# FFN products by one level of Strassen's scheme, and score products pinned in pairs, in a four-block fp32 trunk

## Chip, cores and metric

The kernel runs on one core of one Trainium2 chip, in one launch. The metric is the device time in microseconds of that core; 1996.79 us is the median of three runs (1996.62 to 1997.18).

## What is computed

The input x is 512 tokens of 1024 features in fp32. There are two layers; each adds an FFN, a mixer and a second FFN to x. The mixer of layer 0 is a causal differential attention with 8 heads, that of layer 1 a gated MLP over chunks of 128 tokens (gMLP). Cut to what matters here:

```
def _swiglu_ffn(x, w_gate_up, w_down):          # 1024 x 5632 and 2816 x 1024
    g, u = jnp.split(x @ w_gate_up, 2, axis=-1)
    return (jax.nn.silu(g) * u) @ w_down

for i in range(2):
    x = x + 0.5 * _swiglu_ffn(_rmsnorm(x, ffn1_norm[i]), ffn1_w_gate_up[i], ffn1_w_down[i])
    x = x + mixer(_rmsnorm(x, mix_norm[i]))     # attention in layer 0, gMLP in layer 1
    x = x + 0.5 * _swiglu_ffn(_rmsnorm(x, ffn2_norm[i]), ffn2_w_gate_up[i], ffn2_w_down[i])
```

In the attention, the scores of a head are computed for two components (cc) of 64 features and for blocks of 128 queries, against the keys up to the block's end.

## The kernel before

x lies in SBUF as eight tiles `x[k]` of 128 features by 512 tokens. Products run on TensorE in fp32r form, and each fp32 operand is split into a high part (a copy by ScalarE) and a low part (a subtraction by VectorE), so that `mm3` (L126) issues three matmuls for one product. Names: PE is TensorE, DVE VectorE, ACT ScalarE, POOL GpSimd, SP the engine that issues every load; an f tile is 128 of the 2816 hidden features, a k tile 128 of the 1024 features of x.

The stages follow one another: f0, attention, f1 (layer 0), f2, gMLP, f3 (layer 1). An FFN (`ffn`) goes through two halves of 11 f tiles. For each tile j it loads 1 MB of gate and up weights (`load`, L113), splits them in two pieces of 1024 columns (`split`, L118, with L122 on ACT and L123 on DVE), and multiplies them by the halves `xh`, `xl` of the 8 k tiles, for gate and up: 48 matmuls of 512 columns (L127 to L129). `gated` (L232) scales by the norm's row factor `rb`, takes silu and splits the result h. After a half, 8 down blocks of 704 KB (33 matmuls each) are added to `x[m]` (L285), and in the second half the next norm's `add` makes the new halves and squares (L158, L159, L166, L167).

The norm's factor comes late: `rstd` issues four products with a vector of ones (L173) behind the fourth k tile of the first f tile (the second in f0), and `rows` (L195, L199) turns the factor into a 128x512 tile `rb` on all partitions. Nothing before `gated` needs it.

The framework's scheduler sets the order in each engine's queue by readiness. In the attention and the gMLP, `interleave` (L311) picks the order of tasks by a table of estimated times. `scores` (L481) writes, for one head and one block, three products (L495) per component, alternating between the components, and a mask product (L499); the scheduler is free to move them.

Of the kernel before, what the change touches and what calls it, by code (L numbers as in the profile page):

```python
# [17 lines left out]
P = 128  # L18
# [35 lines left out]
def kernel(  # L54
# [28 lines left out]
    wraw = ctx.enter_context(tc.tile_pool(name="wraw", bufs=2))  # L83
    wsplit = ctx.enter_context(tc.tile_pool(name="wsplit", bufs=5))
# [7 lines left out]
    xh = [acts.tile([P, S], F32R, name=f"xh{k}") for k in range(KT)]  # L92
    xl = [acts.tile([P, S], F32R, name=f"xl{k}") for k in range(KT)]
# [49 lines left out]

    class Norm:


        def __init__(self, layer, kind, name):
            self.g0 = C_GAIN + (layer * 3 + kind) * KT
            self.name = name
            self.acc = stat.tile([P, S], F32, tag="sqacc", name=name + "acc", bufs=1)  # L150

# [28 lines left out]
        def rows(self, r):  # L180
# [6 lines left out]
            for part, half in ((f32(rh), "h"), (rl, "l")):  # L187
# [671 lines left out]
```

## Time and profile before

| | us | 
|---|---|
| median of three runs | 1996.79 |
| the profiled execution, device time | 1996.96 |
| its span, first to last instruction | 1995.2 |
| PE busy | 1984.2 |
| DVE busy | 1032.3 |
| ACT busy | 670.0 |

The span is what the instructions cover; the device time is a little longer. An engine's busy time is the union of its instructions' spans. A busy PE means only that some matmul was under way, since matmuls are pipelined: the starts of two in a row tell the price of one better than a duration does. TensorE's granted clock was 1.0 in every slice, its upper level. A time of landing is that from a DMA's issue to its end.

### The profile page before, as it was taken

What the parts mean: (1) busy time and instruction counts of PE and PEld (TensorE: products, weight loads), DVE (VectorE), ACT (ScalarE), POOL (GpSimd) and SP (SyncE); (2) the same over time, 40 slices, a digit from 0 to 9 for tenths busy, and PEclk for the clock granted to TensorE, in tenths of its full rate; (3) what the DMA queues carried; (4) which work ended last, traced back from release to release, by engine and by line L of the source; (5) the groups of instructions that cost most, each with busy time, mean ns of one, the idle gap of its engine ahead of it and who ended that gap; (6) DMA issues with size and microseconds to landing.
All of it is one profiled execution on the core that took longest, in us unless ns stands there. A gap on an engine that the chain in (4) does not pass through costs nothing.

```text
span 1995.2 us, 22193 instructions
## 1 busy us (share of the span) xinstructions
PE 1984.2 (99%) x9034; PEld 1629.9 (82%) x9034; DVE 1032.3 (52%) x1663; ACT 670.0 (34%) x960; POOL 2.6 (0%) x11
## 2 busy tenths in 40 slices
PE   8999999999999999999999999999999999999999
PEld 7888888877778888888888888888888888888887
DVE  7433444567778443444544334445586564434442
ACT  5222323355554322222423223233333242222321
POOL 0000000000000000000000000000000000000000
PEclk9999999999999999999999999999999999999999
DMA  5223222211112222322322232234332222223222
GB/s 193 99 73 120 100 86 94 105 64 64 55 52 85 89 81 95 126 84 74 127 87 90 88 127 85 79 103 146 115 116 85 89 102 88 83 94 127 85 78 81
DMA packets 32934, 190.34 MB, mean 95 GB/s; under 512 B 3776, under 2 KB 4160, under 8 KB 16576
## 3 DMA queue, kind: packets, MB, share of 16 engines
q1 hardware_dynamic: 32832, 188.93, 27.0%
q8 instruction: 71, 1.16, 0.2%
q14 instruction: 31, 0.25, 0.0%
HBM read 186.82 MB, written 2.10 MB: 95 GB/s over the span
## 4 chain that ended last, share of the span: by engine, by line
PE 98%; DVE 1%; ACT 1%; DMA 0%; SPq 0%; issue 0%; ACTq 0%
PE f2p L127 4%; PE f3p L127 4%; PE f3p L128 4%; PE f2p L129 4%; PE f3p L129 4%; PE f2p L128 4%; PE f1p L127 4%; PE f1p L128 4%; PE f1p L129 4%; PE f0p L127 4%; PE f0p L129 4%; PE f0p L128 4%; PE f3dp L127 2%; PE f2dp L129 2%; PE f1dp L127 2%; PE f0dp L129 2%
## 5 line engine op out<-in xcount | busy, mean ns | idle before, releaser
L235 DVE TENSOR_TENSOR f3g<-f3p,n5rbs 128x512 f32<-128x512 f32 x22 | 15.2, 691 | 58.7 <-PE f3p L129 58.7
L235 DVE TENSOR_TENSOR f1g<-f1p,n2rbs 128x512 f32<-128x512 f32 x22 | 15.2, 692 | 58.7 <-PE f1p L129 57.3
L235 DVE TENSOR_TENSOR f2g<-f2p,n3rbs 128x512 f32<-128x512 f32 x22 | 15.2, 691 | 58.7 <-PE f2p L129 58.7
L235 DVE TENSOR_TENSOR f0g<-f0p,n0rbs 128x512 f32<-128x512 f32 x22 | 15.2, 691 | 55.5 <-PE f0p L129 55.5
L158 ACT ACTIVATE xh<-x,sm 128x512 fp32r<-128x512 f32 x48 | 34.3, 718 | 17.8 <-DVE x L750 9.7
L159 DVE SCALAR_TENSOR_TENSOR xl<-x,sm,xh 128x512 fp32r<-128x512 f32 x48 | 35.6, 746 | 8.5 <-ACT xh L158 8.4
L285 DVE SCALAR_TENSOR_TENSOR x<-f3dp,x 128x512 f32<-128x512 f32 x16 | 11.1, 692 | 40.3 <-PE f3dp L129 40.3
L285 DVE SCALAR_TENSOR_TENSOR x<-f2dp,x 128x512 f32<-128x512 f32 x16 | 11.1, 692 | 29.3 <-PE f2dp L129 29.3
L285 DVE SCALAR_TENSOR_TENSOR x<-f1dp,x 128x512 f32<-128x512 f32 x16 | 11.1, 692 | 29.3 <-PE f1dp L129 29.3
L285 DVE SCALAR_TENSOR_TENSOR x<-f0dp,x 128x512 f32<-128x512 f32 x16 | 11.1, 692 | 29.3 <-PE f0dp L129 29.3
L750 DVE TENSOR_TENSOR x<-gop,x 128x512 f32<-128x512 f32 x24 | 16.5, 689 | 18.4 <-PE gop L129 18.4
L242 ACT ACTIVATE f3hh<-f3u 128x512 fp32r<-128x512 f32 x22 | 13.9, 633 | 28.1 <-DVE f3u L239 28.1
L242 ACT ACTIVATE f2hh<-f2u 128x512 fp32r<-128x512 f32 x22 | 13.9, 632 | 28.0 <-DVE f2u L239 28.0
L243 DVE TENSOR_TENSOR f3hl<-f3u,f3hh 128x512 fp32r<-128x512 f32 x22 | 15.2, 692 | 15.4 <-ACT f3hh L242 15.4
L243 DVE TENSOR_TENSOR f2hl<-f2u,f2hh 128x512 fp32r<-128x512 f32 x22 | 15.2, 692 | 15.4 <-ACT f2hh L242 15.4
L242 ACT ACTIVATE f1hh<-f1u 128x512 fp32r<-128x512 f32 x22 | 13.9, 632 | 27.3 <-DVE f1u L239 27.3
L243 DVE TENSOR_TENSOR f1hl<-f1u,f1hh 128x512 fp32r<-128x512 f32 x22 | 15.2, 692 | 14.7 <-ACT f1hh L242 14.7
L242 ACT ACTIVATE f0hh<-f0u 128x512 fp32r<-128x512 f32 x22 | 13.9, 632 | 26.5 <-DVE f0u L239 26.5
L593 DVE TENSOR_TENSOR x<-aop,x 128x512 f32<-128x512 f32 x32 | 21.5, 684 | 2.4 <-PE aop L129 2.3
L243 DVE TENSOR_TENSOR f0hl<-f0u,f0hh 128x512 fp32r<-128x512 f32 x22 | 15.2, 692 | 14.1 <-ACT f0hh L242 14.0
L730 ACT ACTIVATE gh<-gut 128x512 fp32r<-128x512 f32 x16 | 10.1, 631 | 33.7 <-DVE gut L729 33.7
L689 DVE TENSOR_TENSOR gut<-gup,n4rbs 128x512 f32<-128x512 f32 x16 | 11.0, 685 | 13.4 <-PE gup L129 13.4
(3643 smaller groups left out, 6456.7 us busy)
## 6 DMA issues: line engine op xcount, KB each, us to landing
f1gu<-in_gate_up_dram SPq DMA_DIRECT2D x22, 1024.0 KB, 4.8
f2gu<-in_gate_up_dram SPq DMA_DIRECT2D x22, 1024.0 KB, 4.8
f3gu<-in_gate_up_dram SPq DMA_DIRECT2D x22, 1024.0 KB, 4.8
f0gu<-in_gate_up_dram SPq DMA_DIRECT2D x21, 1024.0 KB, 4.8
f0d<-in_down_dram SPq DMA_DIRECT2D x16, 704.0 KB, 4.0
f1d<-in_down_dram SPq DMA_DIRECT2D x16, 704.0 KB, 4.0
f2d<-in_down_dram SPq DMA_DIRECT2D x16, 704.0 KB, 4.1
f3d<-in_down_dram SPq DMA_DIRECT2D x16, 704.0 KB, 4.1
```

Source lines behind the costliest of these rows:

```text
L127: nc.tensor.matmul(ps, sh, mh, start=start, stop=False)
L128: nc.tensor.matmul(ps, sh, ml, start=False, stop=False)
L129: nc.tensor.matmul(ps, sl, mh, start=False, stop=stop)
L158: nc.scalar.activation(xh[k], x[k], AF.Copy, scale=g)
L159: nc.vector.scalar_tensor_tensor(xl[k], x[k], g, f32(xh[k]), op0=ALU.mult, op1=ALU.subtract)
L235: nc.vector.tensor_tensor(gt, ps[0], rb, op=ALU.mult)
L242: nc.scalar.activation(a, ut, AF.Copy)
L243: nc.vector.tensor_tensor(b, ut, f32(a), op=ALU.subtract)
L285: nc.vector.scalar_tensor_tensor(x[m], pt, 0.5, x[m], op0=ALU.mult, op1=ALU.add)
L593: nc.vector.tensor_tensor(x[m], pt, x[m], op=ALU.add)
L689: nc.vector.tensor_tensor(ut, ps, rr["rb"], op=ALU.mult)
L750: nc.vector.tensor_tensor(x[m], pt, x[m], op=ALU.add)
```

## The change

*FFNs.* An FFN's first two f tiles of each half (`PLAIN` = 2: j = 0, 11, 1, 12) are still computed as before. For the others, tile i of the first half and tile i+11 of the second form a pair, k tiles k and k+4 another, and the two halves of 256 tokens a third. Such a 2×2×2 product is done with seven products in place of eight (Strassen's scheme in its form with shared sums): P1, P2, P6, P7, Q3, Q4 and Q5, on 256 columns. `Weigh` loads the four quarters of the weights a, b, c and d (512 KB each in a pair) and builds the sums: t = a + b on DVE (Q5); then, by DMAs issued from POOL that add to what lies in SBUF, t += c (P6), b += c (P7) and t += d (Q4). Each of the seven is split on ACT and DVE. `multiply` goes through 14 turns (7 products, gate and up) and accumulates them in three banks for each of gate and up: X takes P1, P6, P7 and Q4, Y takes Q5 and Q3, Z takes P2. Partial values are kept (`keep`) and the outputs formed from differences (L448 to L463).

The moving operand needs seven forms of 256 columns: `scaled` makes them for x (scaled by gain and `rb`, which is no longer applied afterwards for these pairs), `sums_of` and `halves_of` (one row of 1792 columns on ACT and one on DVE) make them for x and for h. The down products use the same scheme over pairs of f tiles, of output tiles and token halves, in chunks of 3, 3, 3 and 2 pairs with two parts each; chunks run between the gate and up pairs as soon as their h are there, the last two at the end. All FFN matmuls, with the norm's, are pinned in program order.

*Memory.* Loads are 512 KB in place of 1 MB and four buffers of them; `xh` and `xl` move to a shared pool of three homes; four split buffers instead of five; `QK_BUFS` 5 to 4 and `U_BUFS` 4 to 3.

*Scores.* All products of a group but the first, and the mask products, are pinned in program order.

Matmuls of an FFN go from 1584 of 512 columns to 192 of 512 and 2436 of 256. The last norm's `add`s of a part stand behind that part in program order.

```diff
 O_BUFS = 4
-U_BUFS = 4
-QK_BUFS = 5
+U_BUFS = 3
+QK_BUFS = 4
 BANKS = {"pp": 4, "ps": 3, "po": 1}
+HT = S // 2
+PLAIN = 2
+CHUNKS = ((0, 1, 2), (3, 4, 5), (6, 7, 8), (9, 10))
...
+    fixed = []
+    def matmul(ps, stationary, moving, start, stop, more=False):
+        mm = nc.tensor.matmul(ps, stationary, moving, start=start, stop=stop, skip_group_check=more)
+        if fixed:
+            tc.keep_in_program_order(mm)
...
+    class Weigh:
+        def __init__(self, pool, srcs, n, name):
+            self.n, self.name, self.done = n, name, {}
+            self.raw = {}
+            for q in "abcd":
+                self.raw[q] = t = wraw.tile([P, 1024], F32, tag="raw", name=f"{name}{q}")
+                for dst, src in srcs[q]:
+                    nc.sync.dma_start(t[:, dst], src)
+            t = self.raw["t"] = pool.tile([P, 1024], F32, tag="t", name=f"{name}t")
+            nc.vector.tensor_tensor(t[:, :n], self.raw["a"][:, :n], self.raw["b"][:, :n], op=ALU.add)
+        def more(self, to, by):
+            n = self.n
+            nc.gpsimd.dma_start(self.raw[to][:, :n], self.raw[by][:, :n], accum_op=ALU.add)
+        def take(self, prod):
+            if prod in self.done:
+                return self.done[prod]
+            if prod == "Q5":
+                src = "t"
+            elif prod == "P1":
+                src = "a"
+            elif prod == "P6":
+                self.more("t", "c")
+                self.done["P2"] = split(self.raw["d"], self.n, f"{self.name}P2")
+                src = "t"
+            elif prod == "P7":
+                self.more("b", "c")
+                src = "b"
+            elif prod == "Q4":
+                self.more("t", "d")
+                src = "t"
+            elif prod == "Q3":
+                src = "c"
+            self.done[prod] = split(self.raw[src], self.n, self.name + prod)
+            return self.done[prod]
     def ffn(layer, which, norm, nxt):
...
+        first = which == 0 and layer == 0
+        slot = {"P1": 0, "P2": 1, "Q4": 2, "Q5": 3, "P6": 4, "P7": 5, "Q3": 6}
+        turns = ["Q5a", "P1a", "P1b", "Q5b", "P6a", "P6b", "P2a", "P7a", "P7b", "P2b", "Q4a", "Q4b", "Q3a", "Q3b"]
...
+            def room(name):
+                return fp.tile([P, 8, HT], F32, tag="hr", name=name, bufs=2)
+            def halves_of(h, tiles):
+                hi, lo = tiles
+                nc.scalar.activation(hi, h[:, :7, :], AF.Copy)
+                nc.vector.tensor_tensor(lo, h[:, :7, :], f32(hi), op=ALU.subtract)
+                return tiles
+            def sums_of(h):
+                nc.vector.tensor_tensor(h[:, 3, :], h[:, 7, :], h[:, 2, :], op=ALU.subtract)
+                nc.vector.tensor_tensor(h[:, 4, :], h[:, 3, :], h[:, 0, :], op=ALU.subtract)
+                nc.vector.tensor_tensor(h[:, 5, :], h[:, 0, :], h[:, 7, :], op=ALU.subtract)
+                nc.vector.tensor_tensor(h[:, 6, :], h[:, 1, :], h[:, 4, :], op=ALU.add)
+            def two(t):
+                return t.rearrange("p (a b) -> p a b", a=2)
+            def multiply(weigh, column, pairs, after):
+                acc, n = {}, len(pairs)
+                for turn in turns:
+                    prod, u = turn[:2], turn[2]
+                    wh, wl = weigh.take(prod)
+                    home = {"P": "X", "Q": "Y"}[prod[0]]
+                    home = "Z" if prod == "P2" else "X" if prod == "Q4" else home
+                    fresh = prod in ("P1", "P2", "Q5")
+                    if fresh:
+                        acc[home + u] = bank(f"{weigh.name}{home}{u}", "ps" if home == "Y" else "pp")
+                    ps = acc[home + u][:, :HT]
+                    for i, (hi, lo) in enumerate(pairs):
+                        c0 = column("ab".index(u), i)
+                        mm3(
+                            ps, wh[:, c0], wl[:, c0], hi[:, slot[prod], :], lo[:, slot[prod], :],
+                            fresh and i == 0, i == n - 1, not fresh,
+                        )
+                    after(prod, u, ps)
...
+            def settle(i, h):
+                last = i in CHUNKS[-1]
+                if last or held[0] == 3:
+                    waiting.append((i, h))
+                else:
+                    held[0] += 1
+                    pairs[i] = halves_of(h, form_pair("b", f"{nm}h{i}"))
...
+            def gated(j, ps):
+                i, side = j % FH, j // FH
+                if side == 0:
+                    rooms[i] = room(f"{nm}r{i}")
+                h = rooms[i]
+                gt = fp.tile([P, 4, HT], F32, tag="gt", name=f"{nm}g{j}")
+                g, u = gt[:, :2, :], gt[:, 2:, :]
+                nc.vector.tensor_tensor(g, two(ps[0]), two(rb), op=ALU.mult)
+                nc.scalar.activation(g, g, AF.Silu)
+                nc.vector.tensor_tensor(u, two(ps[1]), two(rb), op=ALU.mult)
+                nc.vector.tensor_tensor(h[:, 1:3, :] if side else h[:, 0:8:7, :], u, g, op=ALU.mult)
+                if side:
+                    sums_of(h)
+                    settle(i, h)
+            def scaled(kp):
+                h = room(f"{nm}x{kp}")
+                for k, dst in ((kp, h[:, 0:8:7, :]), (kp + 4, h[:, 1:3, :])):
+                    nc.vector.scalar_tensor_tensor(
+                        dst, two(x[k]), norm.gain(k), two(rb), op0=ALU.mult, op1=ALU.mult
+                    )
+                sums_of(h)
+                xf.append(halves_of(h, form_pair("a", f"{nm}x{kp}", fp)))
...
+            def gate_up_pair(i):
+                quarter = lambda j, q: [(slice(0, D), gate_up[f, j][:, q * D:(q + 1) * D])]
+                weigh = Weigh(
+                    fp, {"a": quarter(i, 0), "b": quarter(i + FH, 0), "c": quarter(i + FH, 1), "d": quarter(i, 1)},
+                    D, f"{nm}w{i}",
+                )
+                h = room(f"{nm}r{i}")
+                gt = fp.tile([P, 4, HT], F32, tag="gt", name=f"{nm}g{i}")
+                keep = {}
+                def after(prod, u, ps):
...
+                            keep[u] = kept(u, f"{nm}k{i}{u}")
+                        nc.scalar.activation(keep[u][:, ("P1", "P6", "P7").index(prod), :], ps, AF.Copy)
+                    elif prod == "P2":
+                        nc.vector.tensor_tensor(out[:, 0, :], ps, keep[u][:, 0, :], op=ALU.add)
+                    elif prod == "Q4":
+                        if u == "a":
+                            nc.scalar.activation(gt[:, 3, :], ps, AF.Silu)
                         else:
-                            nc.sync.dma_start(out[m], x[m])
+                            nc.vector.tensor_tensor(h[:, 7, :], ps, gt[:, 3, :], op=ALU.mult)
+                    elif prod == "Q3":
+                        nc.vector.tensor_tensor(out[:, 1, :], ps, keep[u][:, 1, :], op=ALU.subtract)
+                        if u == "a":
+                            nc.scalar.activation(gt[:, :3, :], gt[:, :3, :], AF.Silu)
+                        else:
+                            nc.vector.tensor_tensor(h[:, :3, :], h[:, :3, :], gt[:, :3, :], op=ALU.mult)
+                    if prod == "P7":
+                        nc.vector.tensor_tensor(out[:, 2, :], acc_y[u], keep[u][:, 2, :], op=ALU.subtract)
+                    elif prod == "Q5":
+                        acc_y[u] = ps
+                acc_y = {}
...
+            def down_part(chunk):
+                n, k0 = len(chunk), chunk[0]
+                for v in range(2):
+                    ms = {u: (4 * v + 2 * i, 4 * v + 2 * i + 1) for i, u in enumerate("ab")}
+                    block = lambda half, side: [
+                        (slice(i * n * P, (i + 1) * n * P), down[f, half, ms[u][side]][:, k0 * P:(k0 + n) * P])
...
+                        2 * n * P, f"{nm}d{k0}{v}",
+                    )
+                    keep, acc_y = {}, {}
+                    def after(prod, u, ps):
+                        m1, m2 = ms[u]
+                        left, right = slice(0, HT), slice(HT, S)
+                        if prod in ("P1", "P6", "P7"):
+                            if prod == "P1":
+                                keep[u] = kept(u, f"{weigh.name}k{u}")
+                            at = ("P1", "P6", "P7").index(prod)
+                            nc.scalar.activation(keep[u][:, at, :], ps, AF.Copy, scale=0.5)
+                            if prod == "P1":
+                                nc.vector.tensor_tensor(x[m1][:, left], x[m1][:, left], keep[u][:, 0, :], op=ALU.add)
+                            if prod == "P7":
+                                x2 = x[m2]
+                                nc.vector.scalar_tensor_tensor(
+                                    x2[:, right], acc_y[u], 0.5, x2[:, right], op0=ALU.mult, op1=ALU.add
+                                )
+                                nc.vector.tensor_tensor(two(x2), two(x2), keep[u][:, 1:, :], op=ALU.subtract)
+                        elif prod == "Q5":
+                            acc_y[u] = ps
+                        else:
+                            m, cols = {"P2": (m1, left), "Q4": (m1, right), "Q3": (m2, left)}[prod]
+                            nc.vector.scalar_tensor_tensor(
+                                x[m][:, cols], ps, 0.5, x[m][:, cols], op0=ALU.mult, op1=ALU.add
+                            )
+                        if chunk == CHUNKS[-1] and prod in ("Q4", "Q3"):
+                            m = m1 if prod == "Q4" else m2
+                            if nxt is None:
+                                nc.sync.dma_start(out[m], x[m])
+                            else:
...
+            for i in range(PLAIN, FH):
+                gate_up_pair(i)
+                for chunk in CHUNKS[:-2]:
+                    if i == chunk[-1] + 1:
+                        down_part(chunk)
+                        settle_waiting()
+            xf_done.append(1)
+            settle_waiting()
+            down_part(CHUNKS[-2])
+            down_part(CHUNKS[-1])
...
+                        mm = nc.tensor.matmul(
                             pss[cc][:, :L], qT[a][c0, i * P:L], kT[b][c0, :L], start=(a + b == 0), stop=False
                         )
+                        if a + b + cc > 0:
+                            tc.keep_in_program_order(mm)
                 for cc in range(2):
-                    nc.tensor.matmul(pss[cc][:, i * P:L], ident_b, mask_b, start=False, stop=True)
+                    tc.keep_in_program_order(
+                        nc.tensor.matmul(pss[cc][:, i * P:L], ident_b, mask_b, start=False, stop=True)
```

The order on DVE in the middle of f1, before: one f tile's weight splits (L123) and `gated` (L235, L238, L239); `f1gu` is the raw load, `f1p` the product in PSUM.

```order
L123 TENSOR_TENSOR f1w130l<-f1gu_6559,f1w130h 128x1024
L123 TENSOR_TENSOR f1w131l<-f1gu_6559,f1w131h 128x1024
L235 TENSOR_TENSOR f1g_6479<-f1p_6429,n2rbs 128x512
L238 TENSOR_TENSOR f1u_6482<-f1p_6430,n2rbs 128x512
L123 TENSOR_TENSOR f1w140l<-f1gu_6629,f1w140h 128x1024
L239 TENSOR_TENSOR f1u_6482<-f1u_6482,f1g_6479 128x512
```

The same place of the changed kernel, in the pairs 5 and 6: `f1w5`, `f1w6` are their weights (l and h the low and high parts), `f1g` and `f1r` partial results for gate and up, `f1k5` kept values, `Xa` to `Zb` the banks.

```order
L450 TENSOR_TENSOR f1g_8531<-f1w5Za,f1k5a 128x256
L263 TENSOR_TENSOR f1w6t<-f1w6a,f1w6b 128x1024
L463 TENSOR_TENSOR f1g_8531<-f1w5Ya,f1k5a 128x256
L125 TENSOR_TENSOR f1w6Q5l<-f1w6t,f1w6Q5h 128x1024
L463 TENSOR_TENSOR f1r_8530<-f1w5Yb,f1k5b 128x256
L450 TENSOR_TENSOR f1r_8530<-f1w5Zb,f1k5b 128x256
L125 TENSOR_TENSOR f1w6P1l<-f1w6a,f1w6P1h 128x1024
L455 TENSOR_TENSOR f1r_8530<-f1w5Xb,f1g_8531 128x256
L125 TENSOR_TENSOR f1w6P2l<-f1w6d,f1w6P2h 128x1024
L457 TENSOR_TENSOR f1g_8531<-f1w5Ya,f1k5a 128x256
L457 TENSOR_TENSOR f1r_8530<-f1w5Yb,f1k5b 128x256
L461 TENSOR_TENSOR f1r_8530<-f1r_8530,f1g_8531 128x768
```

DVE now forms the next pair's t (L263) and splits its first sums between the rows that combine the present pair's products, and those wait for PE.

The weights of pair 6 on POOL (first three rows, those of pair 5) and SP, with their waits: L267 are the accumulating DMAs, L261 the loads, DMASW the semaphores of POOL's DMAs.

```order
L267 DMA f1w5b<-f1w5c 128x1024 [waits DMAHW6_49,DMASW7_49,DMAHW7_49,DVE_49,Activation_49]
L267 DMA f1w5t<-f1w5c 128x1024 [waits DMASW1_49,DVE_49]
L267 DMA f1w5t<-f1w5d 128x1024 [waits DMASW4_49,DMAHW0_49,DMASW3_49,DVE_49]
L261 DMA f1w6a<-in_gate_up_dram 128x1024 [waits DMAHW5_49,DVE_49]
L261 DMA f1w6b<-in_gate_up_dram 128x1024 [waits DMAHW0_49,DMAHW2_49,DMASW4_49,DVE_49]
L261 DMA f1w6c<-in_gate_up_dram 128x1024 [waits DMASW2_49,DVE_49]
L261 DMA f1w6d<-in_gate_up_dram 128x1024 [waits DMAHW7_49,DMASW3_49,DVE_49]
```

The load of `f1w6b` stands behind the last accumulation of pair 5 (DMASW4), since it takes the place of `f1w5d`; none of these DMAs existed before on POOL, and loads waited for splits alone.

DVE at the start of f1, changed kernel: the last of 57 rows that stand from the first row using `n2rbs` to `f1x3l`, then the next weight splits. `f1x` are forms of x, `f1h1` those of h, L396 is `scaled`, L319 to L322 are `sums_of`, L315 the low halves.

```order
L320 TENSOR_TENSOR f1x_7375<-f1x_7375 128x256
L315 TENSOR_TENSOR f1h1l<-f1r_7283,f1h1h 128x1792
L322 TENSOR_TENSOR f1x_7375<-f1x_7375 128x256
L396 SCALAR_TENSOR_TENSOR f1x_7386<-x_80,sm,n2rbs 128x2x256
L396 SCALAR_TENSOR_TENSOR f1x_7386<-x_84,sm,n2rbs 128x512
L321 TENSOR_TENSOR f1x_7386<-f1x_7386 128x256
L319 TENSOR_TENSOR f1x_7386<-f1x_7386 128x256
L315 TENSOR_TENSOR f1x2l<-f1x_7375,f1x2h 128x1792
L320 TENSOR_TENSOR f1x_7386<-f1x_7386 128x256
L322 TENSOR_TENSOR f1x_7386<-f1x_7386 128x256
L315 TENSOR_TENSOR f1x3l<-f1x_7386,f1x3h 128x1792
L125 TENSOR_TENSOR f1w2P7l<-f1w2b,f1w2P7h 128x1024
```

Before, no row of this kind existed: the halves of x were made ahead, by the norm's `add`, without `rb`. Now the forms of all four k pairs come after it, with rows of h between them.

## Rows read from the trace of the kernel before

**Rows 1.** The page: busy time, share of the span and instructions of each engine.

```profile
PE 1984.2 (99%) x9034; PEld 1629.9 (82%) x9034; DVE 1032.3 (52%) x1663; ACT 670.0 (34%) x960; POOL 2.6 (0%) x11
```

**Rows 2.** The page: the chain that ended last, shares of the span by engine.

```profile
PE 98%; DVE 1%; ACT 1%; DMA 0%; SPq 0%; issue 0%; ACTq 0%
```

**Rows 3.** Busy time by stretch: f0, f1, f2 and f3; the columns are named above.

```profile
core 0: us, PE busy (x) PEld busy (x) DVE busy (x) ACT busy (x) POOL busy (x), PEclk, DMA share, GB/s
5.20:369.20 364.00, 363.01 (x1595) 299.48 (x1595) 177.00 (x235) 120.51 (x158) 0.00 (x0) 1.00 0.31 109
...
632.30:993.30 361.00, 360.83 (x1596) 298.52 (x1596) 170.46 (x219) 111.55 (x145) 0.00 (x0) 1.00 0.28 97
993.30:1353.70 360.40, 360.40 (x1595) 298.53 (x1594) 164.62 (x210) 107.64 (x137) 0.00 (x0) 1.00 0.28 97
...
1630.80:1991.00 360.20, 360.20 (x1594) 298.34 (x1593) 152.53 (x195) 96.84 (x122) 0.00 (x0) 1.00 0.26 92
```

**Rows 4.** Timeline of PE in f0: start us, us, engine line op out<-in count.

```profile
200.10 0.39 PE L128 MATMUL f0p<-xl,f0w111h 128*128 128x512 f32 x1
200.33 0.39 PE L129 MATMUL f0p<-xh,f0w111l 128*128 128x512 f32 x1
200.56 0.39 PE L127 MATMUL f0p<-xh,f0w120h 128*128 128x512 f32 x1
```

**Rows 5.** Timeline of PE in the attention: a lone score group of 256 columns.

```profile
406.81 0.38 PE L495 MATMUL a0s<-qk0Th,qk0Th 64*128 64x256 f32 x1
407.03 0.28 PE L495 MATMUL a0s<-qk0Tl,qk0Th 64*128 64x256 f32 x1
407.15 0.28 PE L495 MATMUL a0s<-qk0Th,qk0Tl 64*128 64x256 f32 x1
407.36 0.23 PE L499 MATMUL a0s<-mask_b,ident_b 128*128 128x128 bf16 x1
```

**Rows 6.** Instructions of line 720 (gMLP) between 1500 and 1502 us.

```profile
L720 PE MATMUL gs<-wT,gv x12: 275/275/275, 1499.8 to 1501.0; 128*128 128x128 f32 x12
```

**Rows 7.** Timeline of PE: a paired score group of 384 columns, first product to mask.

```profile
410.83 0.45 PE L495 MATMUL a0s<-qk0Th,qk0Th 64*128 64x384 f32 x2
...
411.57 0.28 PE L499 MATMUL a0s<-mask_b,ident_b 128*128 128x128 bf16 x2
```

**Rows 8.** Groups by line and shape on DVE: busy, mean ns of one, idle before.

```profile
L159 DVE SCALAR_TENSOR_TENSOR xl<-x,sm,xh 128x512 fp32r<-128x512 f32 x48 | 35.6, 746 | 8.5 <-ACT xh L158 8.4
...
L243 DVE TENSOR_TENSOR f1hl<-f1u,f1hh 128x512 fp32r<-128x512 f32 x22 | 15.2, 692 | 14.7 <-ACT f1hh L242 14.7
...
L458 DVE TENSOR_TENSOR qk1n<-qk1n,qk1rq 128x256 f32<-128x256 f32 x4 | 1.4, 420 | 0.0
...
L123 DVE TENSOR_TENSOR f0w20l<-f0gu,f0w20h 128x1024 fp32r<-128x1024 f32 x1 | 1.2, 1226 | 0.0
```

**Rows 9.** Timeline of DVE at the head of f1, in columns as rows 4.

```profile
641.80 1.22 DVE L123 TENSOR_TENSOR f1w21l<-f1gu,f1w21h 128x1024 fp32r<-128x1024 f32 x1
642.93 0.16 DVE L135 TENSOR_SCALAR n2y<-n2v 128x4 int32<-128x4 int32 x1
```

**Rows 10.** Groups by line and shape on ACT.

```profile
L242 ACT ACTIVATE f1hh<-f1u 128x512 fp32r<-128x512 f32 x22 | 13.9, 632 | 27.3 <-DVE f1u L239 27.3
...
L122 ACT ACTIVATE f1w140h<-f1gu 128x1024 fp32r<-128x1024 f32 x1 | 1.1, 1065 | 4.4 <-PE f1p L128 4.4
```

**Rows 11.** DMA queues and issues: count, KB each, median us from issue to landing.

```profile
q1 hardware_dynamic: 32832, 188.93, 27.0%
...
f1gu<-in_gate_up_dram SPq DMA_DIRECT2D x22, 1024.0 KB, 4.8
...
f1d<-in_down_dram SPq DMA_DIRECT2D x16, 704.0 KB, 4.0
...
bin<-in_b_in_dram SPq DMA_DIRECT2D x4, 256.0 KB, 3.0
...
wT<-in_w_s_dram SPq DMA_DIRECT2D x1, 512.0 KB, 5.7
```

More of the change, by code (lines that the diff above doesn't have):

```diff
@@ L142, in rsqrt, with form_pair @@
         return y
+    def form_pair(home, name, pool=None):
+        pool, bufs = (forms, 3) if pool is None else (pool, 4)
+        return tuple(
+            pool.tile([P, 7, HT], F32R, tag=home + q, name=name + q, bufs=bufs) for q in "hl"
+        )
     class Norm:
@@ L202, in begin @@
     def begin(norm):
-        raw = wraw.tile([P, 2048], F32, tag="raw", name="w0")
+        raws = [wraw.tile([P, 1024], F32, tag="raw", name=f"w0{q}") for q in range(2)]
         cuts = [(0, 1), (1, 2), (2, 4), (4, 6), (6, 8)]
@@ new lines, in scaled @@
+            def scaled(kp):
[6 more added lines that the diff above has]
+                xf.append(halves_of(h, form_pair("a", f"{nm}x{kp}", fp)))
+            plain = [j for i in range(PLAIN) for j in (i, i + FH)]
+            todo = list(range(4))
@@ L276, in ffn @@
+            for at, j in enumerate(plain):
+                if first and at == 0:
+                    parts = begin(norm)
+                else:
                     parts = [
-                        split(raw, 0, DOWN_CUT * P, f"{nm}dw{half}{m}a"),
-                        split(raw, DOWN_CUT * P, (FH - DOWN_CUT) * P, f"{nm}dw{half}{m}b"),
-                    ]
-                    pt = bank(f"{nm}dp{half}{m}", "pp")
-                    for k in range(FH):
-                        wh, wl = parts[k // DOWN_CUT]
-                        c0 = slice((k % DOWN_CUT) * P, (k % DOWN_CUT + 1) * P)
-                        mm3(pt, wh[:, c0], wl[:, c0], hh[k], hl[k], k == 0, k == FH - 1)
@@ L285, in ffn @@
-                    nc.vector.scalar_tensor_tensor(x[m], pt, 0.5, x[m], op0=ALU.mult, op1=ALU.add)
-                    if half == 1:
-                        if nxt is not None:
-                            nxt.add(m)
-                        else:
-                            nc.sync.dma_start(out[m], x[m])
+                        split(load(gate_up[f, j][:, q * D:(q + 1) * D], f"{nm}gu{j}{q}"), D, f"{nm}w{j}{q}")
+                        for q in range(2)
+                    ]
+                ps = [bank(f"{nm}p{j}{u}", "ps" if first and at == 1 else "pp") for u in range(2)]
@@ new lines, in ffn @@
+                for k in range(KT):
+                    wh, wl = parts[k // 4]
+                    for u in range(2):
+                        c0 = slice((k % 4 * 2 + u) * P, (k % 4 * 2 + u + 1) * P)
+                        mm3(ps[u], wh[:, c0], wl[:, c0], norm.xh[k], norm.xl[k], k == 0, k == KT - 1)
+                    if rb is None and at == first:
+                        if k == 3:
+                            r = norm.rstd()
+                        elif k == KT - 1:
+                            rb = norm.rows(r)
@@ L299, in fetch @@
             if i < len(self.srcs) and i not in self.raws:
-                self.raws[i] = load(self.srcs[i][1], 2048, f"{self.srcs[i][0]}r")
+                name, src = self.srcs[i]
+                self.raws[i] = [load(src[:, t * 1024:(t + 1) * 1024], f"{name}r{t}") for t in range(2)]
         def use(self, p):
@@ L305, in use @@
                     self.fetch(q // 2)
[L306 removed]
+                    self.parts[q] = split(self.raws[q // 2][q % 2], 1024, f"{self.srcs[q // 2][0]}s{q % 2}")
                     self.ready[q] = yield 0, [("A", 0.95), ("D", 1.14)], False
```

158 lines of the change are left out of this document (85 added, 73 removed).

## Prediction

> **What bounds the kernel now.** I read the page first, then the chain, the stages, and single instructions. TensorE (PE) is busy for 99% of the span and VectorE (DVE) for half of it [rows 1]; the chain that ended last is 98% PE [rows 2]. A table by stage shows the same at each of the four FFNs, f0 to f3 (364.0, 361.0, 360.4 and 360.2 us), while DVE is busy for 153 to 177 us of each [rows 3]. In an FFN a product starts every 0.227 us [rows 4], and there are 22×2×8×3 + 8×22×3 = 1584 of them: 359.6 us. So an FFN is this stream and nothing else, and a change must shorten it without making a slower one beside it.
>
> **What the change takes from PE.** 192 products of 512 columns stay (43.6 us). The rest becomes products of 256 columns: 9 pairs of 168, and per FFN six down parts of 126 and two of 84, so 2436. Their price is not shown for 128 rows. The 64-row score products of 256 columns start 0.12 us apart where they follow one another [rows 5]; 128-column products, each with a load of its own, 1.2/11 = 0.109 us apart [rows 6]. Half of 0.227 lies between, 0.114. I take 0.12: a pair is 20.2 us, the down parts 15.1 and 10.1, an FFN 335.9, which is 23.7 less than 359.6.
>
> The Trainium skill (TensorE: Matmul & The Clock Gate, Back-to-back issue gap) speaks against this: it has the spacing of a stream set by load and product together and falling only from about 131 to 81 ns between 512 and 128 columns, so that halving the columns would not halve the price; its 131 ns doesn't agree with 0.227 of the rows, and no row here has 128 rows with 256 columns. By its ratio, an estimate of 0.74 at 256 columns, a product would start every 0.17 us and the sum come out near 2380; what would do that here stands as the last rival.
>
> **What it adds to DVE, per pair.** Each of seven sums is split on ScalarE (ACT) and DVE, and t is formed on DVE: eight DVE rows of 1024 columns (1.226), eleven of 256 (0.42), one of 768 and one of 1792 (0.96 and 2.03 by the line through 512 and 1024) [rows 8]. That is 17.4 us, and 15.7 with the 0.08 by which consecutive rows overlap (1.13 from start to start for 1.22) [rows 9]. It fits under 20.2, but barely: DVE is no longer half idle, and each wait in its order counts.
>
> **The loop through t.** One buffer t carries three sums in turn: sum on DVE, split for Q5, accumulate c, split for P6, accumulate d; only then may the next b be loaded (it takes d's place), and the next sum waits for it. Its own rows: 1.23 + 2×(1.06+1.23) = 5.8 [rows 8, 10], a load, two accumulations L. A 512 KB load is 3.6 us by the line through 1024 KB (4.8) and 256 KB (3.0), on which 704 KB (4.0) nearly lies [rows 11]; 384 KB is 3.3. To 9.4 + 2L I add 1.9 for seven hops between engines and queues and for the DVE rows (0.42 to 2.03 each) that stand ahead of a link of the loop: 11.3 + 2L. The down parts have fewer rows between: 4.6 + 3.3 + 0.65 + 2L (768 columns, 384 KB) and 3.3 + 3.0 + 0.3 + 2L (512 columns, 256 KB), so 8.55 and 6.6 + 2L.
>
> L is nowhere in the trace: no DMA of it adds, none is issued by GpSimd (POOL). Bounds for the three sizes: a plain load of the same size, 3.6, 3.3 and 3.0 us; and above, the 512 KB load that took 5.7 us beside others [rows 11]. I take a load of twice the bytes, since adding reads both operands, by the same line: 4.8, 4.2 and 3.6. So a pair takes 20.9, a down part 16.95 or 13.8, all above PE's own time.
>
> The Trainium skill (DMA: Bandwidth & Descriptors, Anatomy of one DMA — SWDGE (gpsimd) path) gives 2.0 us plus the bytes at 436 GB/s, thus 3.2 us for 512 KB; by that the sum is that of the cheap accumulations below. Its rule on reduction (Collectives: The Full Stack, The bandwidth ceiling: the fold count and why AG ≠ RS ≠ AR) has an adding transfer read two sources at half the rate; no run here shows either.
>
> **The start of an FFN.** The scaled forms of x need rb. Its products are pinned behind the 48th product (10.9 us); with about 1 us for the last squares, which rstd now waits for at the 24th, and 0.9 for the two products and the copy, rb is there at 12.8. From there to x3l, which the last products of Q5a need, DVE has 57 rows: 24 of 256 columns, 20 of 512 (8 with a gain at 0.746), 7 of 1024, 6 of 1792: 45 us, 40.4 with overlap [rows 8, 9], and some 2 us waiting for ACT's halves. x3l comes at 55.2; the plain products end at 44.6. PE stands 10.6 us. In f0 rb comes a block later (10.9), with 54 rows and no 1 us: about 17.
>
> **The last chunk.** The norm's adds for the first four x stand on DVE before the second part's weight split: 4×0.746 + 4×0.69 less overlap, 5 us, except in f3.
>
> **At nothing:** the loads in halves of 512 KB, since the same bytes go by a queue that uses 27% of the DMA time [rows 11]; one buffer less of QK and U, hidden by PE's stream; if that cover fails, the attention grows by 0 to 5 us. The scores: a lone group of 256 columns took 0.55 us to its mask product (1.10 for two), a paired one of 384 only 0.74 for both [rows 5, 7]. That is 0.36 for each of 32 groups at most, 11.5, and 0 at least; I take 5, as some are paired already.
>
> **Sum.** An FFN: 43.6 + 1 + 10.6 + 9×20.9 + 6×16.95 + 2×13.8 + 5 = 377.6. Against the rows: f1 +16.6, f2 +17.2, f3 (no adds) +12.4, f0 +23.4 (6.4 more at the start, 1 less, and the 4.4 of its head, 364.0−359.6, stay). That is +70; with −5 for the scores +65, on the profiled execution's 1996.96: 2062. That execution is 0.2 us above the median of the runs. About 0.2% (4 us) is what a measurement can tell from no change.
>
> **Rivals.**
> - *Cheap accumulations.* L as a plain load (3.6, 3.3, 3.0): the loop of a pair falls to 18.5, under PE's 20.2, those of the down parts to 15.15 and 12.6. An FFN is 43.6 + 1 + 10.6 + 181.8 + 90.9 + 25.2 + 5 = 358.1; f1 −2.9, f2 −2.3, f3 −7.1, f0 +3.9, with the scores −13: 1984. For it: the sources lie in SBUF; against: two operands.
> - *The cover holds everywhere.* PE binds, and the start and the norm's adds hide too. It needs L ≤ (20.2−11.3)/2 = 4.4 in pairs and (15.1−8.55)/2 = 3.3 in the down parts of 768; those of 512 stay 2.5 over their 10.1, twice in each FFN: 4×(−23.7+5) − 5 = −80, 1917. For it: DVE and ACT have half their time or more free now [rows 1], and the two starts of my sum are worked out on paper from an order, with every row at its full price; against it: the 57 rows stand in that order, rows of h among them. This is the side opposite to my forecast.
> - *Slow accumulations.* At 5.7 and, in the same ratio, 5.0 and 4.3 (POOL's issue, loads beside it) pairs take 22.7, the down parts 18.55 and 15.2: an FFN 406.2, and the four +45, +46, +41 and +52: with the scores 2176. It decides from about L = 5.2 on.
> - *The halving isn't one.* Loads take 1629.9/9034 = 0.18 us each [rows 1]; they overlap products of 0.227, and if they set the pace of the small ones, an FFN is 43.6 + 2436×0.18 = 482, the four together +487: 2479. Against it: the 0.109 of rows 6, with loads as long.
>
> **How the numbers follow.** Forecast 0.45 (2010 to 2115, L from 4.1 to 5.2), slow accumulations 0.18, cheap ones 0.12, cover holds 0.2, no halving 0.05. Faster by over 0.2% are the cheap ones, the cover, and 0.02 of other ways: 0.34; within 0.2%: 0.05; slower 0.61. The range leaves out the half of the cover that lies under 1915, the no-halving case and the part of the slow one beyond 2185: 0.1 + 0.05 + 0.05, so 1915 to 2185; the forecast's own range is 2010 to 2115.
>
> **What would show it.** In the profile after: PE pitch 0.12 in pairs; landings of the accumulating DMAs near 4.8 for 512 KB; pair period near 21 with PE idle released by splits of Q5 or P6 whose chain goes to POOL's queue; a gap of about 11 us in f1 between the plain products and Q5a, released by x3l; DVE busy about three quarters of an FFN. I am wrong if PE is idle under 5 us an FFN (cover holds), if L is above 5.5, or if pitch is not near 0.12.

## The result and the profile after

The changed kernel takes 2233.04 us (median of four runs, 2228.55 to 2242.71) where the kernel before took 1996.7: a ratio of 1.119, 95% interval 1.1153 to 1.1226, 236 us slower. It lies above the range that was given, and beyond the rival of slow accumulations, 2176. The page and its chain, against [rows 1, 2]:

```profile
PE 1995.6 (89%) x13210; PEld 1818.4 (81%) x13210; DVE 1547.3 (69%) x2571; ACT 1015.2 (45%) x1544; POOL 183.4 (8%) x215
...
DMA 2%; PE 1%; DVE 1%; issue 0%; ACT 0%; POOL 0%; DVEq 0%; POOLq 0%; ACTq 0%
```

PE, busy for 99% before, is busy for 89%. The chain, followed back from the end, shows DMAs at its head (the accumulations of f3, by line), but it breaks off after some 4% of the span, so the stages have to tell the rest. Busy time by stretch: f0, attention, f1, f2, gMLP and f3, in the columns of [rows 3]:

```profile
5.50:427.40 421.90, 364.57 (x2628) 346.05 (x2629) 294.41 (x448) 199.58 (x296) 44.19 (x51) 0.94 0.59 145
427.40:689.30 261.90, 261.06 (x1381) 200.25 (x1380) 201.47 (x565) 144.48 (x293) 0.00 (x0) 1.00 0.22 71
689.30:1112.30 423.00, 364.81 (x2639) 346.70 (x2638) 292.79 (x438) 195.11 (x286) 44.05 (x51) 0.94 0.55 133
1112.30:1534.00 421.70, 363.56 (x2631) 346.06 (x2630) 289.85 (x434) 191.34 (x280) 44.07 (x51) 0.94 0.56 137
1534.00:1813.20 279.20, 278.90 (x1301) 232.90 (x1301) 184.30 (x264) 96.76 (x121) 5.48 (x1) 1.00 0.35 113
1813.20:2227.60 414.40, 362.63 (x2639) 346.36 (x2638) 283.13 (x423) 185.13 (x269) 44.07 (x51) 0.94 0.56 135
```

All of the loss is in the FFNs: 57.9, 62.0, 61.3 and 54.2 us. PE stands still for 52 to 58 us in each, and its granted clock is no longer 1.00. Attention and gMLP are within 2.2 us of before. Yet the products cost what was forecast, 0.12 us each where nothing waits. Timeline of PE in pair 9 of f1 (start us, us, ...):

```profile
999.93 0.28 PE L132 MATMUL f1w9Xa<-f1x1h,f1w9P6l 128*128 128x256 f32 x1
1000.05 0.28 PE L132 MATMUL f1w9Xa<-f1x2h,f1w9P6h 128*128 128x256 f32 x1
1000.17 0.28 PE L132 MATMUL f1w9Xa<-f1x2l,f1w9P6h 128*128 128x256 f32 x1
```

What is new is on POOL. DMA issues in pair 5 of f1 (us to landing at the end), and the queues:

```profile
q1 hardware_dynamic: 78768, 188.95, 25.7%
q0 software_dynamic: 29376, 91.24, 23.4%
...
f1w5b<-f1w5c POOLq DMA_DIRECT2D x1, 512.0 KB, 6.0
f1w5t<-f1w5c POOLq DMA_DIRECT2D x1, 512.0 KB, 7.6
...
f1w5t<-f1w5d POOLq DMA_DIRECT2D x1, 512.0 KB, 4.5
```

Over all weight groups, t += d lands in 4.5, 3.9 and 4.5 us (medians for 512, 384 and 256 KB) and t += c in 6.1, 6.2 and 4.4; for the two larger sizes t += c takes longer because b += c was issued just ahead on the same queue, as the fourth run below shows. The loop of t can be followed row by row, here from pair 5 of f1 to pair 6:

```profile
855.60 1.22 DVE L263 TENSOR_TENSOR f1w5t<-f1w5a,f1w5b 128x1024 f32<-128x1024 f32 x1
859.53 0.86 POOL L267 DMA_DIRECT2D f1w5t<-f1w5c  x1 [1.32 <-DVE f1w5Q5l L125]
867.24 1.06 ACT L124 ACTIVATE f1w5P6h<-f1w5t 128x1024 fp32r<-128x1024 f32 x1 [4.19 <-DMA f1w5t<-f1w5c]
869.85 0.86 POOL L267 DMA_DIRECT2D f1w5t<-f1w5d  x1 [9.46 <-DVE f1w5P6l L125]
874.42 0.33 SPq L261 DMA_DIRECT2D f1w6b<-in_gate_up_dram  x1
878.47 1.22 DVE L263 TENSOR_TENSOR f1w6t<-f1w6a,f1w6b 128x1024 f32<-128x1024 f32 x1
```

Every step begins within 0.5 us of the end of the one before it, and from sum to sum 22.9 us go by.

The start of f1 is the other loss. The rows show ACT, then DVE, then PE, whose first products of the pair wait for the forms of x:

```profile
731.94 1.71 ACT L314 ACTIVATE f1h0h<-f1r 128x1792 fp32r<-128x1792 f32 x1 [2.73 <-PE f1p L132]
```

```profile
733.68 2.03 DVE L315 TENSOR_TENSOR f1h0l<-f1r,f1h0h 128x1792 fp32r<-128x1792 f32 x1 [2.67 <-ACT f1h0h L314]
...
736.75 1.41 DVE L396 SCALAR_TENSOR_TENSOR f1x<-x,sm,n2rbs 128x512 f32<-128x512 f32 x2
...
756.66 2.03 DVE L315 TENSOR_TENSOR f1x3l<-f1x,f1x3h 128x1792 fp32r<-128x1792 f32 x1 [1.76 <-ACT f1x3h L314]
```

```profile
759.12 0.41 PE L132 MATMUL f1w2Ya<-f1x3h,f1w2Q5l 128*128 128x256 f32 x1
759.33 0.41 PE L132 MATMUL f1w2Xa<-f1x0h,f1w2P1h 128*128 128x256 f32 x1
```

The plain products end at 738.5; x3l comes at 758.7, 20 us later. The forms of x0 were made by 720, those of x1 begin only at 736.75, behind h0l and one weight split. And when the products run, they start 0.21 us apart: PE's granted clock was 0.97 before, 0.63 while it waited, and 0.50 (the lower level, 1.2 GHz) in the first 4 us after:

```profile
689.30:738.50 49.20, 46.73 (x203) 38.32 (x202) 37.78 (x62) 18.87 (x22) 1.72 (x2) 0.97 0.34 97
738.50:759.00 20.50, 3.95 (x12) 2.33 (x12) 18.35 (x27) 8.39 (x6) 0.86 (x1) 0.63 0.21 52
759.00:763.00 4.00, 4.00 (x20) 4.00 (x21) 0.00 (x0) 0.38 (x1) 0.00 (x0) 0.50 0.00 0
```

### The profile page after: what moved, and what is told of

Read it like the earlier page. It is cut to its first block, busy times and chain, and to the rows that moved or that the text cites. A ratio compares the mean times of both kernels' runs of the same rounds, so it can differ in the third digit from the quotient of the medians.

```text
span 2231.3 us, 33836 instructions
## 1 busy us (share of the span) xinstructions
PE 1995.6 (89%) x13210; PEld 1818.4 (81%) x13210; DVE 1547.3 (69%) x2571; ACT 1015.2 (45%) x1544; POOL 183.4 (8%) x215
## 5 line engine op out<-in xcount | busy, mean ns | idle before, releaser
L267 POOL DMA_DIRECT2D f1w2b<-f1w2c x1 | 0.9, 862 | 297.2 <-ACT f1g L385 297.2
L267 POOL DMA_DIRECT2D f3w2b<-f3w2c x1 | 0.9, 877 | 291.4 <-ACT f3g L385 291.4
L978 DVE TENSOR_TENSOR gst<-gs,bs 128x512 f32<-128x512 f32 x16 | 11.0, 688 | 8.8 <-PE gs L973 8.8
L973 PEld LDWEIGHTS gs<-wT,gv 128*128 128x128 f32 x128 | 16.1, 191 | 0.9
L973 PE MATMUL gs<-wT,gv 128*128 128x128 f32 x128 | 16.2, 274 | 0.0
L923 ACT ACTIVATE gv<-gv 128x512 f32<-128x512 f32 x16 | 10.1, 629 | 10.2 <-DVE gv L922 10.1
L943 ACT ACTIVATE gut<-gut,sm 128x512 f32<-128x512 f32 x16 | 11.5, 719 | 5.8 <-DVE gut L942 5.8
L984 DVE TENSOR_TENSOR gl<-gut,gh 128x512 fp32r<-128x512 f32 x16 | 11.0, 688 | 4.2 <-ACT gh L983 4.2
L459 ACT ACTIVATE f0g<-f0g 128x768 f32<-128x768 f32 x9 | 7.6, 843 | 13.3 <-DVE f0g L457 13.3
L459 ACT ACTIVATE f2g<-f2g 128x768 f32<-128x768 f32 x9 | 7.6, 843 | 13.3 <-DVE f2g L457 13.3
L959 DVE SCALAR_TENSOR_TENSOR gv<-gv,lny,lnb 128x512 f32<-128x512 f32 x16 | 11.6, 746 | 1.3 <-DMA lnb<-in_ln_b_dram 1.3
L958 DVE SCALAR_TENSOR_TENSOR gv<-gv,lnmv,lng 128x512 f32<-128x512 f32 x16 | 11.5, 743 | 1.4 <-DMA lng<-in_ln_g_dram 1.4
L982 DVE TENSOR_TENSOR gut<-gut,gst 128x512 f32<-128x512 f32 x16 | 11.0, 689 | 0.7
L924 DVE BATCH_NORM_STATS2 lnst<-gv 128x6 f32<-128x512 f32 x16 | 10.8, 684 | 0.1
```

The lines of the kernel that those rows point to most:

```text
L459: nc.scalar.activation(gt[:, :3, :], gt[:, :3, :], AF.Silu)
L924: nc.vector.bn_stats(st[:, n, b, :], z)
L943: nc.scalar.activation(ut, ut, AF.Gelu, bias=sm[:, C_BU + c:C_BU + c + 1])
L958: nc.vector.scalar_tensor_tensor(vv, vv, mv[:, n, 0:1], gr, op0=ALU.subtract, op1=ALU.mult)
L959: nc.vector.scalar_tensor_tensor(vv, vv, rr["y"][:, n:n + 1], lr, op0=ALU.mult, op1=ALU.add)
L973: nc.tensor.matmul(ps[:, n * P:(n + 1) * P], v32[n][:, c * P:(c + 1) * P], wT[:, g, :], start=True, stop=True)
```

## The experiments

The theories: A, the two accumulations in the loop of t set the pairs and down parts; B, DVE's order does; C, PE's low clock costs by itself; D, formed after the eighth run, a ring of buffers sets the start. The table shows f1 in parts, in us from a part's first product to that of the next part; the text below refers to it.

| f1 | plain | first pair | two pairs after down parts | other pairs, mean | six down parts of 3 | last two | all |
|---|---|---|---|---|---|---|---|
| changed kernel | 49.3 | 41.6 | 43.4 | 22.7 | 113.6 | 39.0 | 423.1 |
| sums on DVE (2) | 49.2 | 42.2 | 49.0 | 20.2 | 95.2 | 26.1 | 382.6 |
| + three plain tiles (5) | 71.0 | 43.1 | 49.0 | 20.2 | 95.1 | 26.1 | 385.1 |
| + own room, three split buffers (9) | 72.5 | 21.1 | 46.0 | 21.1 | 103.7 | 28.9 | 377.5 |
| shared room, four split buffers (12) | 74.8 | 20.2 | 43.7 | 20.2 | 95.5 | 26.6 | 361.5 |

**1 to 4. What do the accumulations cost?** The one line of `more` (L267) is changed:

```diff
-            nc.gpsimd.dma_start(self.raw[to][:, :n], self.raw[by][:, :n], accum_op=ALU.add)
+            nc.gpsimd.tensor_tensor(self.raw[to][:, :n], self.raw[to][:, :n], self.raw[by][:, :n], op=ALU.add)
```

> The three sums of each weight group are made by additions on GpSimd itself in place of accumulating DMAs; nothing else is changed. Theory A (the two accumulations in the loop of t, 4.6 us alone and 5.5 to 7.1 behind another, set the pairs and down parts, and PE's low clock after the waits makes them dearer): the waits of PE inside pairs and down parts go, an FFN falls from 422 to about 375 us, the kernel to 2045 (2020 to 2090), unless an addition of 1024 columns takes over 4 us there. Theory B (DVE's order and ScalarE's set them, whatever the sums cost): 2200 or more.

Measured: 2192.6 us (1.0978, 1.0957 to 1.1000). Neither A's 2045 nor quite B's 2200. An addition takes 2.5 us, less than the DMA, but holds DVE up. Timelines of POOL and DVE in pair 5 of f1:

```profile
859.18 2.51 POOL L267 TENSOR_TENSOR f1w5t<-f1w5t,f1w5d 128x1024 f32<-128x1024 f32 x1 [6.06 <-DVE f1w5P6l L125]
```

```profile
859.01 0.42 DVE L319 TENSOR_TENSOR f1r<-f1r 128x256 f32<-128x256 f32 x1
859.35 2.62 DVE L321 TENSOR_TENSOR f1r<-f1r 128x256 f32<-128x256 f32 x1
861.89 0.41 DVE L320 TENSOR_TENSOR f1r<-f1r 128x256 f32<-128x256 f32 x1
```

A row of 0.42 us takes 2.62 and ends 0.3 us behind the addition. DVE's busy time rises from 1547 to 1796 us with the same 2571 rows. So this run doesn't tell A from B; the next one does (the same line on `nc.vector`):

> The same three sums as additions on VectorE, 1.23 us each for 1024 columns. Theory A: the loop of t shrinks to about 15 us, but DVE has 15.7 + 3.4 = 19.1 us of work in a pair of 20.2, so part of the gain is lost again: 2050 to 2120. Theory B: DVE is the bound already, and 3.4 us more per weight group give 4 x 17 x 3 = 200 us more, 2400.

2071.88 us (1.0375, 1.0354 to 1.0395), 161 less than the changed kernel, with 204 rows more on DVE. The pairs that don't follow a down part, but for the first, take PE's 20.16 us, and four of six down parts 15.1 to 15.2. A holds, B falls. What is left on PE in f1 is the start and splits late behind other DVE rows:

```profile
PE f1w2Ya L132 <- ACT f1x2h L314: 8.0, 1, 8.0
PE f1d91Xa L132 <- DVE f1d91P1l L125: 4.0, 1, 4.0
PE f1w2Ya L132 <- ACT f1x1h L314: 3.4, 1, 3.4
```

The third run drops `accum_op`: copies in place of sums.

> The accumulating DMAs become plain copies of the same bytes on the same queue (the sums are left out: t and b hold copies, so the output differs). If reading two operands makes them slow, a copy of 512 KB lands in 3.5 us or less and the kernel falls under 2180; if the time is the queue's (issue, order, the loads beside it), they land in 4.5 us or more and the time stays within 1% of 2233.

2050.74 us (1.0269, 1.0248 to 1.0289): the adding makes the transfers long, not the queue by itself. Copies of 512 KB land in about 3 us, where an accumulation alone takes 4.5; and t's copy, issued 2 us behind b's, isn't held up:

```profile
f1w6b<-f1w6c POOLq DMA_DIRECT2D x1, 512.0 KB, 3.4
f1w6t<-f1w6c POOLq DMA_DIRECT2D x1, 512.0 KB, 2.9
f1w6t<-f1w6d POOLq DMA_DIRECT2D x1, 512.0 KB, 2.9
```

The fourth wraps the DMA in `tc.keep_in_program_order(...)`:

> The accumulating DMAs are pinned in program order, so that t += c is issued ahead of b += c, not behind it. Theory A says that t += c then lands in about 4.6 us where it took 5.5 to 7.1: 1.5 us less in each of 17 loops of 4 FFNs, 60 to 100 us less with the lower clock's share, 2130 to 2170. If it lands no earlier, or if P7 then waits for b += c, within 1% of 2233.

2146.43 us (1.0744, 1.0728 to 1.0760), 87 less. t += c now lands in 4.7 us (median for 512 KB, 6.1 before) and b += c, behind it, in 8.4:

```profile
f1w6t<-f1w6c POOLq DMA_DIRECT2D x1, 512.0 KB, 4.6
f1w6b<-f1w6c POOLq DMA_DIRECT2D x1, 512.0 KB, 7.6
f1w6t<-f1w6d POOLq DMA_DIRECT2D x1, 512.0 KB, 5.2
```

So of some 160 to 180 us that the accumulations cost, about half was the order of two DMAs on one queue.

**5 to 8. The start, the scores and the clock.** The second run's kernel with one constant changed (and `and todo` where the list of forms may be empty):

```diff
-PLAIN = 2
+PLAIN = 3
```

> On top of the sums on VectorE (2072 us): three f tiles of each half stay plain in place of two, 21.8 us more of products that need no scaled form of x, for 1.6 us more of PE work per FFN. If the start costs what its gap shows (19 to 20 us of waiting for the forms of x, and 2 more at PE's low clock), 13 to 18 us go per FFN: 2000 to 2020. If the forms only come later by as much (each plain tile adds rows of h to DVE's queue ahead of them), 2060 or more.

2076.42 us (1.0401, 1.0386 to 1.0417): nothing won. The plain products end 22 us later, and the gap moved along with them, 21.6 us long. From rb to x3l it is now 75 us where it was 52, and DVE idles for 19 of them. So it was neither DVE's volume nor the time since `rb`. DVE shows the same neighbours as in the changed kernel:

```profile
713.37 2.03 DVE L315 TENSOR_TENSOR f1h0l<-f1r,f1h0h 128x1792 fp32r<-128x1792 f32 x1 [3.72 <-ACT f1h0h L314]
716.45 1.41 DVE L396 SCALAR_TENSOR_TENSOR f1x<-x,sm,n2rbs 128x512 f32<-128x512 f32 x2
```

The kernel before with the pinned scores alone (the diff's last hunk):

> The kernel before with the pinned score products alone. My sum: 5 us less (0 to 11), 1992. The stage table of the changed kernel says 1 to 2 us less (the attention took 261.9 us after, 263.1 before), 1995.5.

1993.95 us (0.9985, 0.9976 to 0.9995): 2.9 us less, between the two values.

For the clock, `fill(150)` stands ahead of the first pair:

```diff
+            def fill(n):
+                ps = bank(nm + "fill", "po")
+                for q in range(n):
+                    matmul(ps[:, :P], ones_r, ones_r, True, True)
```

> The changed kernel with 150 products of 128 columns that need nothing (into a bank that nobody reads) between the plain products and the first pair, about 16.5 us, in the gap of some 19 us in which PE waits for the forms of x. Theory C (PE's low clock behind each wait costs by itself): the granted clock stays at its upper level there, the first products of the pair start 0.12 us apart and not 0.21, and 2 to 3 us go per FFN: 2221 to 2226. If the clock costs nothing, no change, or up to 8 us more where the filling stands in the way of Q5a.

2232.21 us (1.1183, 1.1162 to 1.1204): no change. Locally C is right: the clock stays at its upper level in the stretch of the filling and in the first 4 us of the pair,

```profile
743.90:760.60 16.70, 16.70 (x152) 16.70 (x150) 16.29 (x25) 7.03 (x6) 0.86 (x1) 1.00 0.27 64
760.60:764.60 4.00, 2.15 (x16) 1.75 (x16) 2.02 (x1) 1.39 (x1) 0.00 (x0) 1.00 0.00 0
```

and filling and pair take 39.3 us where the pair alone took 41.6. In the profiled executions f1 is 3.4 and f2 6.0 us shorter, f0 4.2 and f3 1.0 longer, and either kernel's runs lie 11 to 14 us apart, so this run can't tell the 7 to 12 us that were expected in all from nothing. What the clock costs in the pairs and down parts, where the loop of t sets the pace, was not tried separately.

The eighth run has sums on DVE, three plain tiles, `settle_waiting()` called behind the next pair's `multiply`, and `nxt.add` of the first part spread over the turns of the second.

> Sums on VectorE, three plain tiles, and two edits of order: the waiting halves of h stand behind the next pair's products and not before its first splits, and the norm's adds of the last chunk's first part are spread over the turns of the second. By the traces of the second run the first edit is worth 2 x 4.3 us per FFN, the other up to 5 us in three FFNs: with the start's gain 1950 to 1985, faster than before. If DVE is the bound (19 us of work in 20.2), only the start's gain is left: 2000 to 2020.

2064.35 us (1.0338, 1.0322 to 1.0353), above both ranges, which counted on the start's gain that the fifth run didn't find. The first order edit took the pairs after down parts from 24.5 to 21.85 us, about three fifths of what I gave it; the second made the last part dearer (16.0 to 19.05 in f1) and was dropped.

**9 to 12. The ring of buffers.** Reading the code beside the rows of the fifth run: `room` has two buffers. r0 takes one until h0's halves are made, x0 the other, then, when x0's halves are made, the second tile's r1 (written at 729.87 us in the changed kernel), so x1 waits for r0's. h0's halves go to a home ("b") that the norm's halves of k tiles 0 to 2 hold until the last plain tile has used them. So x1 waits for the last plain tile, however many there are.

```diff
-                h = room(f"{nm}x{kp}")
+                h = fp.tile([P, 8, HT], F32, tag="xr", name=f"{nm}x{kp}", bufs=1)
```

> The fifth run's kernel (sums on VectorE, three plain tiles, 2076 us) with one edit: the forms of x get a room of their own, paid for with one split buffer less (four to three). Theory D (a ring of buffers sets the start: the second form of x waits for the room that r0 holds, r0 for its halves, these for a home that the last plain product frees, so the start's gap of 20 us follows the plain products however many there are): the gap behind the plain products goes from 20 to under 4 us and the low clock with it, some 18 us per FFN, 2000 to 2015. If DVE's volume sets the start, or if three split buffers stall every pair, no gain or a loss.

2046.19 us (1.0244, 1.0227 to 1.0261), 30 us less than the fifth run, but not the 2000 to 2015 of the forecast. The first pair of f1 falls from 43.1 to 21.1 us: theory D holds. But with three split buffers (`wsplit`, four before) PE waits for splits, about 1 us more in each pair that doesn't follow a down part and 8.6 in the six down parts of 3:

```profile
PE f1w4Xa L132 <- DVE f1w4P6l L125: 1.6, 1, 1.6
PE f1d00Xa L132 <- DVE f1d00P6l L125: 1.1, 1, 1.1
PE f1w5Xa L132 <- DVE f1w5P6l L125: 0.7, 1, 0.7
```

> The same with the waiting halves of h put behind the next pair's products, which took the two pairs behind a down part from 24.5 to 21.85 us in the eighth run: 5 us per FFN less than the ninth, 1980 to 1995.

2048.95 us (1.0259, 1.0243 to 1.0274): nothing; with three split buffers, splits are late whatever stands ahead of them (22.3 and 23.9 us in those pairs).

> The tenth with b += c alone as an accumulating DMA (it has eight turns to land), t += c and t += d on VectorE: 1.1 us less of DVE's work per weight group. If DVE's load still costs anything in the down parts, 5 to 15 us less than the tenth; if the DMA's loads beside it cost as much, no change; if P7 waits for it, more.

2053.86 us (1.0287, 1.0271 to 1.0303), no gain: 1.1 us less of DVE's work per weight group didn't shorten the whole, so DVE's volume is not shown to be what was short.

The last run keeps four split buffers and lets the forms of x use the room that `kept` values need later (`sq` gets one buffer):

```diff
+            def shared(name):
+                return fp.tile([P, 8, HT], F32, tag="xk", name=name, bufs=1)
             def kept(u, name):
-                return fp.tile([P, 3, HT], F32, tag="keep" + u, name=name)
+                if u == "a":
+                    both[:] = [shared(name)]
+                return both[0][:, 0:3, :] if u == "a" else both[0][:, 3:6, :]
```

> Sums on VectorE, three plain tiles, the halves of h behind the next pair's products, and a room of 8 KB for the forms of x that the kept values of the pairs use later, so that the four split buffers stay (paid for with one buffer for squares). Theory D: the ninth run lost by three split buffers (1 us in each pair, 1 to 2 in the down parts, 14 us per FFN) what it won at the start (22 us in f1); with four, an FFN is 382 - 22 = 360, the kernel 1965 to 1990, below the kernel before. If the shared room makes pairs wait for one another, or the single buffer for squares the norms, 2000 or more.

1981.77 us, 0.9925 (0.9911 to 0.9939): faster than both kernels: 0.75%, or 15.5 us, less than the one before, and 2.9 us of that is what the pinned scores gave alone in the sixth run. Its page:

```profile
PE 1921.3 (97%) x12922; PEld 1753.4 (89%) x12922; DVE 1699.2 (86%) x2739; ACT 1006.4 (51%) x1508; POOL 2.9 (0%) x11
```

## Why the prediction was wrong

*What held.* Slower, and by the mechanism that was given most weight: the loop of t, 11.3 + 2L in pairs, 8.55 + 2L and 6.6 + 2L in down parts. With the measured pairs of landings (6.1 + 4.5, 6.2 + 3.9, 4.4 + 4.5) it gives 22.0, 18.6 and 15.4; the pairs of f1 but the first took 22.4 in the mean, the six down parts 18.9. Single pairs took from 20.2 to 26.1, and most of PE's waits in them end with a copy of a partial value on ACT (L448, L495: 24.8 of 39.3 us behind the first pair of f1), which stands in ACT's queue, mostly behind a split that waits for an accumulation, and not with the splits of Q5 or P6 that the prediction named. A product of 256 columns starts 0.12 us after the one before, and where the sums come in time a pair takes 20.16, as written. The spacing that the Trainium skill gives (TensorE: Matmul & The Clock Gate, Back-to-back issue gap), by which, as an estimate, halving the columns would save only a quarter, isn't what this stream does: 0.227 and 0.12. The scores: 5 was forecast, 2.9 measured, in the range of 0 to 11.

*The term that was mis-sized: L.* I took 4.8, 4.2 and 3.6, the landing of a load of twice the bytes. Alone, an accumulation takes 4.5, 3.9 and about 3.3, so a load of twice the bytes was a good guess for the size. The Trainium skill (Collectives: The Full Stack, The bandwidth ceiling: the fold count and why AG ≠ RS ≠ AR) has the reducing step of a collective read two sources and run at about half the rate; here an accumulation takes 1.55 times a copy (4.5 against 2.9), which goes the same way, but no run shows that the second read is the reason. What I left out is the queue: b += c is ready first and goes ahead of t += c, which the order of POOL on record showed. In f1, the first pair aside, that is 8×1.1 + 6×1.7 + 2×1.6 = 22 us; the fourth run, which took the queue's order away, won 87 us, or 22 for each FFN.

*The step that failed: the start.* "PE stands 10.6 us" rested on 57 rows at full speed. In f1, plain products and first pair took 90.9 us; by the sum they were 43.6 + 1 + 10.6 + 20.9 = 76.1, so 14.8 too little. In f2, f3 and f0 the same sums were 11.9, 10.4 and 3.9 too little. rb came 17.6 us in, not 12.8, and DVE waited 9.2 us in those rows, not 2. What my sum left out is a cycle of buffers that no sum of durations contains; the ninth and twelfth runs show it, but with three plain tiles. In the ninth, x3l follows rb by 39.4 us, in the changed kernel by 51.7. With rb at 17.6 that would put x3l some 8 us behind the plain products, not 20. So with two plain tiles the cycle is worth about 12 us: an estimate, since two plain tiles with a room of their own were not run. It doesn't explain the 4.7 us by which the plain stretch itself was longer than forecast (49.3 for 44.6). f1 took 423.1 us where 377.6 were forecast: of those 45.5, L is 22 and the start 14.8; some 3.5 are in the other eight pairs (179.5 for 8×22.0), 1.7 in the six down parts (113.6 for 6×18.65) and 3.1 in the last two parts (39.0 for 2×15.45 + 5), all more than the loop gives; what of this is the lower clock was not separated.

*The rivals.* "Cheap accumulations" (1984) is what the third run's pairs show, 20.16 us each; it took 2051, and some 41 of those 67 us are at the starts of its four FFNs (13.3 in f1: 88.7 for 75.4); "slow accumulations" (2176) had the sum of the two landings nearly right (11.4 for 10.7 in pairs), though not for its reasons, and the same start as my forecast; the cover held in no FFN of the changed kernel, and the halving is one.

## What to carry to other kernels

A saving on the bound engine is worth no more than the slowest loop beside it: write that loop out with its queue, and ask which transfer is issued just ahead of the one that it waits for. When a gap keeps its length while the work before it grows, look for a buffer, not for volume: follow each ring from the tile that waits to the last reader of its place. Memory moves the bound: the buffer that ended one wait here took a split buffer from each pair, and the change paid only when both fitted.

## What the runs showed that I had not expected

- An addition of 1024 columns on POOL takes mostly 2.4 to 2.8 us, and a DVE row that reads two operands from SBUF meanwhile stands until it ends (0.42 became 2.62 us). Accumulating by DMA does not do this: DVE's splits stayed at 1.22 us.
- An accumulating DMA of 512 KB with nothing ahead of it took 4.5 us against 2.9 for a copy, and 0.86 us of POOL for each issue.
- PE's granted clock falls to its lower level in waits of this kind, and products behind them start 0.21 us apart. In the changed kernel the mean was 0.953, in the twelfth run 0.994.
